# Hybrid encoder on one Trainium2 core: first transfers from two queues, the first slice split on ACT and VectorE, the second layer's first chunks in two passes, new ranks

## The chip, the cores and the metric

The kernel runs on one core of a Trainium2 chip. The metric is the device time of one execution in microseconds. Five engines work side by side, each with its own in-order list of instructions: TensorE (PE, with its weight loads shown apart as PEld), VectorE (DVE), ScalarE (ACT), GpSimd (POOL) and SyncE (SP), which here only issues DMAs. They wait for each other through semaphores.

## The reference

The trunk has two layers, called layer 0 and layer 1 below, on x of 512 positions by 1024 features, float32. Each layer does this:

```python
h = rmsnorm(x, g_attn[l])
proj = jnp.einsum('bsd,dc->bsc', h, w_in[l])            # 2304 columns
qa, ka, va, qb, kb, vb = jnp.split(proj, offs, axis=-1)
...  # q, k: RMSNorm by head, then rotary
ya = windowed_gqa_sink(qa, ka, va, sink[l])              # 8 q heads, 2 kv heads, dim 64, +-128
yb = diff_attention(qb, kb, vb, lam)                     # 4 heads, two softmaxes each
yb = rmsnorm(yb, subln[l]) * (1.0 - lambda_init)
y = jnp.concatenate([ya.reshape(B, S, SWA_Q), yb.reshape(B, S, DIFF_V)], axis=-1)
x = x + jnp.einsum('bsm,md->bsd', y, w_out[l])
h = rmsnorm(x, g_ffn[l])
gate, val = jnp.split(jnp.einsum('bsd,df->bsf', h, w_up[l]), 2, axis=-1)
gate = centred_dwconv(gate, conv_w[l], conv_b[l])        # width 3
x = x + jnp.einsum('bsf,fd->bsd', jax.nn.silu(gate) * val, w_down[l])
```

## The kernel before

**Arithmetic.** Every operand of a product is kept as two float32r parts: hi is a rounded copy (made by ACT), lo is what is left (made by VectorE, a few halves by GpSimd). A product is three matmuls, hi·hi, hi·lo and lo·hi, added up in one PSUM bank (`mm3`). This holds for activations and for weights, so each weight unit that arrives by DMA into a `wr` buffer (two of them) is cast by ACT into a `wh` buffer and subtracted into a `wl` buffer (three of each).

**Layout.** x lies transposed in SBUF as eight slices x0 to x7 of 128 features by 512 positions. `Norm.add` makes hi and lo of slice k, scaled by the norm's gain (`na_h`, `na_l`; in the feed-forward half `nf_h`, `nf_l`). The norm's 1/rms per position is applied later, to the product's result; `Norm.squares` adds up the squares of the eight slices (ACT squares, VectorE or GpSimd adds, `na_sum`), and `Norm.rms` makes the factor from it with four small matmuls (`na_ss`), VectorE and GpSimd.

**Stages of a layer.** The input projection is cut into nine chunks of 256 columns (`CHUNKS`, line 30). The first two, akv (keys and values of group A) and aq0, are made together by `first_product`: for each slice k it multiplies all four blocks of 128 positions into four PSUM banks (`pj_akq`), so that it can begin when the first slice and the first part of the weight are there. The other chunks come one after another (`project`): for two pairs of position blocks, all eight slices. Each q or k chunk then passes through `qk_track` and `qk_out`: ACT evacuates the bank (`raw_`), squares it, VectorE reduces, GpSimd takes a power, the rotary steps follow (VectorE in group A, GpSimd in group B), TensorE transposes (`tr_`, into the one bank `at`), and ACT and VectorE copy the two parts out. Group A's attention has eight steps (`sc_a` scores, softmax on VectorE and ACT, `pt_a` transposes of the weights, `pv_a`), group B's sixteen (`sc_b`, `wt_b`, `yb`, then `ss_yb` and `rt_yb` for its norm). The output projection (`wo`) runs in three passes, each adding its bank to x on VectorE (`add_x`), which frees the bank. The feed-forward half follows in two parts (`up`, `dn`).

**The order of the work.** The program order of every engine is made by a planner, `Machine`. Each piece of work is a Python generator ("track") that yields instructions or conditions. The planner holds a model of each engine's free time (`Op.cost`) and of when each operand is ready (`when`, with `NEAR` as the time from a result to a reader on TensorE or GpSimd), and puts next the instruction that could start earliest; among those within a small margin the lowest rank wins. The ranks are in `RK`: "w" weight casts (three values, by how many units are ready), "x" and "xl" the residual adds, "evac" the evacuation of projections, "kv", "qka", "qkb" the q and k tracks, "a" and "b" the attention groups, "bn" group B's norm, "nsq" the squares of the feed-forward norm. The projections and products of the main line (`filler`) have rank 1000, so that TensorE takes attention work when it is ready and projections else.

**The start.** `loads` issues on SP: `cols` (the gains and other parameters by column), then x0, the first part of w_first, x1, the second part, and so on in turn to x7, then the identity, the next weights, the rotary table, the mask and the row parameters. TensorE meanwhile does two float32 warm-up matmuls. On ACT, `first_norm` makes `na_h` of slice 0, `squares` its square, and `first_weights` the cast of the weight's first part (`wh_f`); VectorE makes `na_l` and `wl_f`.

Almost all instructions are issued on one helper line (`put`, line 248 before, 250 after), so the rows of the profile are told apart by tile names.

Of the kernel before, what the change touches and what calls it, by code (L numbers as in the profile page):

```python
# [17 lines left out]
P = 128  # L18
# [11 lines left out]
CHUNKS = ("akv", "aq0", "bq0", "bv0", "aq1", "bk0", "bv1", "bk1", "bq1")  # L30
# [4 lines left out]
AQ_TAGS = ("mm", "at")  # L35
HOLD = 0.05
SWITCH = {True: 0.2, False: 0.085}
NEAR = {"PE": 0.2, "POOL": 0.079}
# [5 lines left out]
RK = {"w": (25, 45, 4), "qkb": (8, 1), "x": 25, "xl": 18, "a": 400, "b": 12, "evac": 1, "qka": 1, "kv": 36,  # L44
      "bn": -2, "nsq": 36, "av": -4, "bv": -4}


class Op:
# [16 lines left out]
    def cost(self, writes, reads):  # L65
# [80 lines left out]
class Machine:  # L146
# [73 lines left out]
    def put(self, op, start):  # L220
# [10 lines left out]
        if op.eng == "SP":  # L231
# [46 lines left out]
class Queue:  # L278
# [13 lines left out]
def kernel(  # L292
# [96 lines left out]

    def w_load(first):  # L390
# [7 lines left out]
    def w_high(first):  # L398
        for i in range(first, len(units)):
            src, (k, n), kind = units[i]  # L400
            yield lambda: len(raws) > i
            yield m.room("wh")
            hi = new("wh", f"wh{i}", [P, k, n])
# [3 lines left out]
    def w_low(first):  # L407
        for i in range(first, len(units)):
            src, (k, n), kind = units[i]
            yield lambda: len(his) > i  # L410
            yield m.room("wl")
            lo = new("wl", f"wl{i}", [P, k, n])
# [9 lines left out]
            ready.append((hi, lo))  # L422
# [22 lines left out]
    class Norm:  # L445
# [7 lines left out]
        def add(self, k):  # L453
# [3 lines left out]
            yield act.activation(self.hi[k], x_sb[k], AF.Copy, scale=g)  # L457
# [85 lines left out]
    def first_product(l, norm, on_banks):  # L543
        banks = []
        for k in range(NK):
            if l == 0:
                yield m.has(f"fw{k}")
            if k % 2 == 0:
                yield unit_there
                w = next_unit()  # L550
            yield m.has(f"{norm.name}{k}")
            for t in range(NT):
                if k == 0:
                    yield roomy(FIRST_TAGS)
# [774 lines left out]
```

## Time and profile before

| what | value |
|---|---|
| median of 3 runs | 1201.58 us (1200.91 to 1202.31) |
| the profiled execution | 1201.83 us |
| its span, first to last instruction | 1200.0 us |
| granted clock, mean over the span | 0.998 |
| chain that ended last | PE 87%, DVE 9%, ACT 2%, POOL 1%, issue 1% |

A row of the timeline has start and duration in us, the engine, the line, the operation, out<-in, the shapes, and xN where N instructions were merged; in brackets stands how long the engine was idle before, and what ended that. A row of the waits has who waited for whom, the total in us, the number of waits and the longest. Matmuls overlap in the records, so one lasts longer than the distance to the next; the rate is read from distances. In rows by stretch of time, each engine has its busy time and its count.

### The profile page before, as it was taken

What the parts mean: (1) busy time and instruction counts of PE and PEld (TensorE: products, weight loads), DVE (VectorE), ACT (ScalarE), POOL (GpSimd) and SP (SyncE); (2) the same over time, 40 slices, a digit from 0 to 9 for tenths busy, and PEclk for the clock granted to TensorE, in tenths of its full rate; (3) what the DMA queues carried; (4) which work ended last, traced back from release to release, by engine and by line L of the source; (5) the groups of instructions that cost most, each with busy time, mean ns of one, the idle gap of its engine ahead of it and who ended that gap; (6) DMA issues with size and microseconds to landing.
All of it is one profiled execution on the core that took longest, in us unless ns stands there. A gap on an engine that the chain in (4) does not pass through costs nothing.

```text
span 1200.0 us, 16742 instructions
## 1 busy us (share of the span) xinstructions
PE 1185.3 (99%) x6452; PEld 1008.6 (84%) x6452; DVE 739.8 (62%) x1329; ACT 556.9 (46%) x977; POOL 226.6 (19%) x282
## 2 busy tenths in 40 slices
PE   8999999999999999999999999999999999999998
PEld 6998988888888888888888899888888888888887
DVE  6887799775554335454458877897755533455532
ACT  5587766454333123333436777665433321233321
POOL 2614360111100000111235144501111100011000
PEclk9999999999999999999999999999999999999999
DMA  6221121132322233322332111211323223323232
GB/s 223 71 71 36 54 71 36 54 106 88 106 84 91 93 119 91 103 84 80 103 116 69 53 54 36 71 53 36 123 88 106 81 91 97 118 89 106 76 117 87
DMA packets 33327, 102.90 MB, mean 86 GB/s; under 512 B 3936, under 2 KB 4192, under 8 KB 33248
## 3 DMA queue, kind: packets, MB, share of 16 engines
q1 hardware_dynamic: 33248, 101.84, 27.2%
q8 instruction: 50, 0.82, 0.3%
q14 instruction: 29, 0.24, 0.1%
HBM read 99.73 MB, written 2.10 MB: 85 GB/s over the span
## 4 chain that ended last, share of the span: by engine, by line
PE 87%; DVE 9%; ACT 2%; POOL 1%; issue 1%; DMA 0%; SPq 0%; DVEq 0%; ACTq 0%; POOLq 0%
PE up L248 40%; PE dn L248 20%; PE wo L248 5%; PE pj_akq L248 3%; PE pj_bk L248 3%; PE pv_a L248 2%; PE sc_b L248 2%; PE pj_aq L248 2%; PE pj_bq L248 2%; PE yb L248 1%; PE pt_a L248 1%; DVE wl L248 1%; PE pj_bv L248 1%; DVE mx_b L248 1%; PE sc_a L248 1%; PE wt_b L248 1%
## 5 line engine op out<-in xcount | busy, mean ns | idle before, releaser
L248 ACT CAST wh<-wr 128x1024 fp32r<-128x1024 f32 (+2 forms) x200 | 193.3, 966 | 378.6 <-PE up L248 183.9
L248 DVE TENSOR_TENSOR wl<-wr,wh 128x512 fp32r<-128x512 f32 (+3 forms) x240 | 230.1, 967 | 110.0 <-ACT wh L248 109.8
L248 PE MATMUL up<-nf_h,wh 128*128 128x512 f32 x704 | 274.3, 390 | 0.0
L248 PE MATMUL up<-nf_h,wl 128*128 128x512 f32 x704 | 273.9, 389 | 0.0
L248 PE MATMUL up<-nf_l,wh 128*128 128x512 f32 x704 | 273.9, 389 | 0.0
L248 PE MATMUL dn<-act,wh 128*128 128x512 f32 x704 | 216.8, 389 | 0.0
L248 POOL TENSOR_TENSOR cv<-cv,rb 128x512 f32<-128x512 f32 x44 | 57.6, 1309 | 521.3 <-ACT cv L248 521.3
L248 PEld LDWEIGHTS dn<-act,wh 128*128 128x128 f32 x704 | 132.2, 188 | 27.4
L248 PEld LDWEIGHTS up<-nf_h,wh 128*128 128x128 f32 x704 | 132.2, 188 | 27.3
L248 PEld LDWEIGHTS up<-nf_h,wl 128*128 128x128 f32 x704 | 132.2, 188 | 27.3
L248 PEld LDWEIGHTS up<-nf_l,wh 128*128 128x128 f32 x704 | 132.2, 188 | 27.2
L248 PE MATMUL dn<-act,wl 128*128 128x512 f32 x352 | 136.9, 389 | 0.0
L248 DVE TENSOR_TENSOR gp<-up,rb 128x512 f32<-128x512 f32 x44 | 30.4, 693 | 109.7 <-PE up L248 106.2
L248 DVE TENSOR_TENSOR cv<-cv,up 128x512 f32<-128x512 f32 x44 | 30.2, 687 | 83.4 <-POOL gp L248 79.0
L248 PEld LDWEIGHTS dn<-act,wl 128*128 128x128 f32 x352 | 66.1, 188 | 13.7
L248 DVE SCALAR_TENSOR_TENSOR cv<-gp,cols,cv 128x512 f32<-128x512 f32 x88 | 66.6, 761 | 5.3 <-ACT cv L248 0.9
L248 DVE TENSOR_TENSOR x<-x,dn 128x512 f32<-128x512 f32 x32 | 22.0, 687 | 74.1 <-PE dn L248 74.1
L248 ACT ACTIVATE cv<-cv 128x512 f32<-128x512 f32 x44 | 27.8, 632 | 83.7 <-DVE cv L248 83.6
L248 ACT ACTIVATE e_b<-sc_b,mx_b,rqb 128x512 f32<-128x512 f32 x64 | 49.7, 784 | 10.2 <-DVE mx_b L248 9.6
L248 ACT ACTIVATE so_a<-so_a,ng_a,rqa 128x256 f32<-128x256 f32 (+1 forms) x64 | 41.4, 651 | 11.6 <-DVE ng_a L248 11.6
L248 DVE TENSOR_REDUCE mx_b<-sc_b 128x2 f32<-128x1024 f32 x32 | 38.1, 1217 | 3.8 <-PE sc_b L248 3.7
L248 PE MATMUL pj_bv<-wh,na_h 128*128 128x256 f32 x128 | 37.8, 295 | 0.2 <-ACT raw_bq L248 0.2
(213 smaller groups left out, 2191.0 us busy)
## 6 DMA issues: line engine op xcount, KB each, us to landing
wr<-w_up SPq DMA_DIRECT2D x88, 512.0 KB, 3.5
wr<-w_in SPq DMA_DIRECT2D x28, 512.0 KB, 3.5
wr<-w_down SPq DMA_DIRECT2D x32, 384.0 KB, 3.0
wr<-w_down SPq DMA_DIRECT2D x32, 320.0 KB, 2.8
wr<-w_out SPq DMA_DIRECT2D x16, 512.0 KB, 3.5
x<-xT SPq DMA_DIRECT2D x8, 256.0 KB, 5.2
prob_f<-w_first SPq DMA_DIRECT2D x8, 256.0 KB, 5.2
wr<-w_first SPq DMA_DIRECT2D x4, 512.0 KB, 3.4
```

The source lines that it names most:

```text
L248: getattr(self.raw[op.eng], op.name)(*op.args, **op.kw)
```

## The change

- The DMA of the first part of the first weight is issued by ACT, ahead of its table load; SP issues x0 first, then `cols`, then the rest as before. The planner now takes 0.45 us for a DMA issue on any engine (0.33 before, on SP).
- The high part of slice 0 is made by VectorE (`tensor_scalar`) instead of ACT.
- In layer 0 the square of slice k waits, in the planner, for the split weight part k.
- In the first two slices of layer 0's first product, the matmuls are ordered by part (hi·hi of all four blocks, then hi·lo, then lo·hi) instead of by block.
- In layer 1 the first product goes through the slices twice: first for position blocks 0 and 1, then for 2 and 3. Its four weight units are held until the second pass has read them.
- The third and fourth weight units of each layer lie in `pair` buffers (which hold the q and k chunks later) instead of `wh` and `wl`.
- Chunk bq0 moves from third to seventh; the chunk aq1 may no longer use the bank `at`.
- NEAR for TensorE goes from 0.2 to 0.053 us, and most of the ranks change.

```diff
-CHUNKS = ("akv", "aq0", "bq0", "bv0", "aq1", "bk0", "bv1", "bk1", "bq1")
+CHUNKS = ("akv", "aq0", "bv0", "aq1", "bk0", "bv1", "bq0", "bk1", "bq1")
-AQ_TAGS = ("mm", "at")
+AQ_TAGS = ("mm",)
-NEAR = {"PE": 0.2, "POOL": 0.079}
+NEAR = {"PE": 0.053, "POOL": 0.079}
-RK = {"w": (25, 45, 4), "qkb": (8, 1), "x": 25, "xl": 18, "a": 400, "b": 12, "evac": 1, "qka": 1, "kv": 36,
-      "bn": -2, "nsq": 36, "av": -4, "bv": -4}
+RK = {"w": (25, 45, 4), "qkb": (39, 1), "x": 2, "xl": 8, "a": 60, "b": 1, "evac": 60, "qka": 12, "kv": 4,
+      "bn": 4, "nsq": 42, "av": -4, "bv": -2}
...
+        if self.name == "dma_start":
+            return 0.45, 0.0
...
+    def w_tag(i, tag):
+        return "pair" if i % (len(units) // depth) in (2, 3) else tag
...
-            yield act.activation(self.hi[k], x_sb[k], AF.Copy, scale=g)
+            if self.first and k == 0:
+                yield dve.tensor_scalar(out=self.hi[k], in0=x_sb[k], scalar1=g, scalar2=None, op0=ALU.mult)
+            else:
+                yield act.activation(self.hi[k], x_sb[k], AF.Copy, scale=g)
...
-                yield m.has(f"{self.name}{k}")
+                yield m.has(f"{self.name}{k}", *([f"fw{k}"] if self.first else []))
...
     def loads():
+        first_w.append(new("prob", "prob_f0", [P, 2, S], F32))
+        yield act.dma_start(first_w[0][:, 0], units[0][0][:, 0])
+        yield sync.dma_start(x_sb[0], x_v[:, 0])
+        yield sync.dma_start(cols[:, :, :N_COL], col_par)
         yield act.activation(warm, ones, AF.Copy, scale=ones)
-        yield sync.dma_start(cols[:, :, :N_COL], col_par)
+        m.flags.add("x0")
         for k in range(NK):
+            if k == 0:
+                continue
...
     def first_product(l, norm, on_banks):
-        banks = []
-        for k in range(NK):
...
+        w = []
+        for blocks in ((0, 1, 2, 3),) if l == 0 else ((0, 1), (2, 3)):
+            banks = []
+            for k in range(NK):
+                if blocks[0] == 0:
...
+                        w.append(next_unit())
...
+                for v in zip(*ops) if l == 0 and k < 2 else ops:
+                    yield Batch(list(v))
+                if blocks[-1] == NT - 1 and k % 2:
+                    done_with(u)
+            for i in range(0, len(blocks), 2):
+                on_banks(banks[i:i + 2], blocks[i] // 2)
```

More of the change, by code (lines that the diff above doesn't have):

```diff
@@ L401, in w_high @@
             yield lambda: len(raws) > i
-            yield m.room("wh")
-            hi = new("wh", f"wh{i}", [P, k, n])
+            th = w_tag(i, "wh")
+            yield m.room(th)
+            hi = new(th, f"wh{i}", [P, k, n])
             yield act.copy(hi, raws[i])
@@ L410, in w_low @@
             yield lambda: len(his) > i
-            yield m.room("wl")
-            lo = new("wl", f"wl{i}", [P, k, n])
+            tl = w_tag(i, "wl")
+            yield m.room(tl)
+            lo = new(tl, f"wl{i}", [P, k, n])
             raw, hi = raws[i], his[i]
@@ L432, in done_with @@
     def done_with(u):
-        m.drop("wh", u[0])
-        m.drop("wl", u[1])
+        m.drop(u[2], u[0])
+        m.drop(u[3], u[1])
     def mm3(acc, a, b, start, stop):
@@ L531, in first_weights @@
             if k % 2 == 0:
-                yield m.room("wh")
-                yield m.room("wl")
-                u = (new("wh", f"wh_f{k}", [P, 2, S]), new("wl", f"wl_f{k}", [P, 2, S]))
+                th, tl = w_tag(k // 2, "wh"), w_tag(k // 2, "wl")
+                u = (new(th, f"wh_f{k}", [P, 2, S]), new(tl, f"wl_f{k}", [P, 2, S]), th, tl)
                 ready.append(u)
-            hi, lo = (v[:, k % 2] for v in u)
+            hi, lo = (v[:, k % 2] for v in u[:2])
             yield act.copy(hi, raw[:, k % 2])
@@ L543, in first_product @@
     def first_product(l, norm, on_banks):
-        banks = []
-        for k in range(NK):
[L546 to L554, printed above, removed]
-                    banks.append(any_bank(f"pj{l}_akq_{t}", FIRST_TAGS))
-                yield from mm3(banks[t][2], (norm.hi[k][:, t * P:(t + 1) * P], norm.lo[k][:, t * P:(t + 1) * P]),
-                               (w[0][:, k % 2], w[1][:, k % 2]), k == 0, k == NK - 1)
-                if k == NK - 1 and t % 2:
-                    on_banks(banks[t - 1:t + 1], t // 2)
-            if k % 2:
-                done_with(w)
+        w = []
[3 more added lines that the diff above has]
+                if blocks[0] == 0:
+                    if l == 0:
+                        yield m.has(f"fw{k}")
+                    if k % 2 == 0:
+                        yield unit_there
+                        w.append(next_unit())
+                    yield m.has(f"{norm.name}{k}")
+                u = w[k // 2]
+                ops = []
+                for i, t in enumerate(blocks):
+                    if k == 0:
+                        yield roomy(FIRST_TAGS)
+                        banks.append(any_bank(f"pj{l}_akq_{t}", FIRST_TAGS))
+                    ops.append([pe.matmul(banks[i][2], lhsT=a[k][:, t * P:(t + 1) * P], rhs=u[j][:, k % 2],
+                                          start=n + k == 0, stop=n == 2 and k == NK - 1)
+                                for n, (a, j) in enumerate(((norm.hi, 0), (norm.hi, 1), (norm.lo, 0)))])
+                for v in zip(*ops) if l == 0 and k < 2 else ops:
[4 more added lines that the diff above has]
+                on_banks(banks[i:i + 2], blocks[i] // 2)
     def warm_up():
```

10 lines of the change are left out of this document (5 added, 5 removed).

## The prediction

> **What bounds the kernel now.** I read the page first, then the busy time by stage, then the waits of TensorE, then the timelines of the three places where it waits. The page, and two of the stages (span, then busy time and count of PE, PEld, DVE, ACT, POOL, then granted clock, DMA share, GB/s):
>
> ```profile
> span 1200.0 us, 16742 instructions
> PE 1185.3 (99%) x6452; PEld 1008.6 (84%) x6452; DVE 739.8 (62%) x1329; ACT 556.9 (46%) x977; POOL 226.6 (19%) x282
> ...
> 31.50:240.50 209.00, 206.42 (x1522) 185.29 (x1521) 177.70 (x421) 138.58 (x306) 70.42 (x57) 1.00 0.18 55
> 240.50:601.40 360.90, 360.90 (x1602) 299.16 (x1601) 181.37 (x226) 131.28 (x169) 39.53 (x73) 1.00 0.31 96
> ```
>
> TensorE has work from end to end. The feed-forward stage of layer 0, 360.9 us, has no gap, the change leaves its order alone, and layer 1's is its copy. So a time can change only by three things: the time before the first product, the clock during it, and the moments at which TensorE stands still in the attention stages. The change alters no count of matmuls. All named waits of TensorE, with their totals:
>
> ```profile
> PE pj_akq L248 <- ACT wh_f L248: 2.1, 1, 2.1
> PE wo L248 <- DVE x L248: 2.1, 3, 0.8
> PE tr_ka L248 <- DVE qal L248: 1.4, 1, 1.4
> PE pt_a L248 <- DVE p_a L248: 1.3, 4, 0.4
> PE tr_bq L248 <- POOL raw_bq L248: 1.2, 2, 1.0
> PE warm_up L248 <- POOL unit L358: 1.0, 1, 1.0
> PE rt_yb L248 <- POOL rr_yb L248: 0.5, 2, 0.3
> PE pj_akq L248 <- DVE wl_f L248: 0.2, 1, 0.2
> PE pj_bv L248 <- ACT raw_bq L248: 0.2, 1, 0.2
> PE tr_qa L248 <- DVE ka L248: 0.2, 1, 0.2
> ```
>
> Without the first product's two and the warm-up's, 6.9 us of waits remain; that is all that "ranks anew", the chunk order and the two passes can win between them. The start, in order of time:
>
> ```profile
> 0.73 1.28 ACT L248 ACT_TABLE_LOAD   x1 [0.73 <-PEq L1325]
> 0.74 0.67 SPq L248 DMA_DIRECT2D cols<-col_par  x1
> 0.95 3.48 PE L248 MATMUL warm_up<-unit 128*128 128x512 f32 x4 [0.95 <-POOL unit L358]
> 1.46 0.58 SPq L248 DMA_DIRECT2D x<-xT  x1
> 2.09 0.42 SPq L248 DMA_DIRECT2D prob_f<-w_first  x1
> 4.76 0.72 ACT L248 ACTIVATE na_h<-x,cols 128x512 fp32r<-128x512 f32 x1 [2.44 <-DMA x<-xT]
> 5.39 0.61 ACT L248 ACTIVATE na_sum<-x 128x512 f32<-128x512 f32 x1
> 5.91 0.60 ACT L248 CAST wh_f<-prob_f 128x512 fp32r<-128x512 f32 x1
> 6.54 0.69 DVE L248 TENSOR_TENSOR wl_f<-prob_f,wh_f 128x512 fp32r<-128x512 f32 x1 [0.28 <-ACT wh_f L248]
> 6.56 0.51 PE L248 MATMUL pj_akq<-wh_f,na_h 128*128 128x512 f32 x1 [2.14 <-ACT wh_f L248]
> 7.29 0.71 PE L248 MATMUL pj_akq<-wl_f,na_h 128*128 128x512 f32 x1 [0.22 <-DVE wl_f L248]
> ...
> 547.05 54.40 PE dn L248 x240
> ```
>
> Three ACT steps stand in a row (the slice's high part, its square, the weight's cast) before the first matmul at 6.56. The last row gives the pitch of a 512-column matmul, 54.40 / 240 = 0.227 us.
>
> **The change part by part.** *The start.* ACT and DVE before:
>
> ```order
> L248 ACT_TABLE_LOAD
> L248 ACTIVATE unit<-unit 128x1
> L248 ACTIVATE na_h_104<-x_66,cols 128x512
> L248 ACTIVATE na_sum<-x_66 128x512
> L248 CAST wh_f_105<-prob_f_100 128x512
> ```
>
> ACT now; x_66 and prob_f_82 are the first slices of x and of the weight:
>
> ```order
> L250 DMA prob_f_82<-w_first 128x512
> L250 ACT_TABLE_LOAD
> L250 ACTIVATE unit<-unit 128x1
> L250 CAST wh_f_105<-prob_f_82 128x512
> L250 ACTIVATE na_sum<-x_66 128x512
> ```
>
> DVE now, from its first instruction:
>
> ```order
> L250 TENSOR_TENSOR wl_f_106<-prob_f_82,wh_f_105 128x512
> L250 TENSOR_SCALAR na_h_104<-x_66,cols 128x512
> L250 SCALAR_TENSOR_TENSOR na_l_121<-x_66,cols,na_h_104 128x512
> L250 SCALAR_TENSOR_TENSOR na_l_138<-x_67,cols,na_h_124 128x512
> L250 TENSOR_TENSOR wl_f_106<-prob_f_82,wh_f_105 128x512
> ```
>
> The high part moved from ACT to DVE, but behind the weight's low part: "at once" is in truth cast, low part, high part. When the data come is bounded by these answers (min, median, max to landing, of x, the first weights and cols):
>
> ```profile
> DMA to landing us min/median/max: 3.2/5.2/5.8
> ...
> DMA to landing us min/median/max: 3.4/5.2/5.9
> ...
> DMA to landing us min/median/max: 2.5/2.5/2.5
> ...
> 3.50:4.00 0.50, 0.50 (x2) 0.00 (x0) 0.00 (x0) 0.00 (x0) 0.00 (x0) 1.00 1.07 377
> ```
>
> The weight is issued at 0.73 by ACT instead of at 2.09; its landing is bounded by 3.2 and 3.9 us behind that (3.4, the least of its own rows, plus 0.5 for sharing: 256 KB at 377 GB/s is 0.7 us, and x is under way at the same time). I take 4.2. Cols, now second on SP at about 1.4, land 2.5 to 3.4 later, by 4.8. Then cast 0.60 to 4.85, low part 0.69 to 5.5. The high part on DVE, with a scalar per partition, has no row of its shape before: a 128x512 product of another form took 0.69 (wl_f above), so 0.3 to 0.69; I take 0.45, nearer its simpler arithmetic. First matmul at about 6.0 against 6.56: **-0.56** (0 if data come 0.6 later, -0.9 if 0.3 earlier). The four high matmuls and then the four with the low part fill 8 x 0.227 = 1.8 us, in which the slice's low part is made, so the stall from 6.56 to 7.29 (0.73 - 0.227 = 0.50) is gone: **-0.50**. The squares held back cost nothing: the sum of squares moves from behind 54 product matmuls to behind 66, and its readers, the evacuations at the end of the first product, come 30 matmuls (6.8 us) later still. ACT's new DMA issue (0.42 to 0.67 by SP's rows) puts its table load 0.7 later, to end at 2.7, before any data.
>
> The Trainium skill ("Trainium Kernel Development and Optimization", Key Constraints) says that DMAs of several queues share the same 16 DMA engines and interleave, so that a second queue saves only issue time. That speaks against a gain from two queues; by it only the one issue, 0.42 us, would be won, and my 0.56 stands mostly on the dropped ACT steps.
>
> *The clock.*
>
> ```profile
> 7.00:7.50 0.50, 0.28 (x2) 0.21 (x2) 0.24 (x2) 0.50 (x2) 0.00 (x0) 0.91 1.22 266
> 7.50:8.00 0.50, 0.50 (x2) 0.40 (x2) 0.50 (x1) 0.50 (x2) 0.00 (x0) 0.50 0.90 262
> ...
> 10.00:11.00 1.00, 1.00 (x4) 0.81 (x3) 1.00 (x3) 1.00 (x3) 0.00 (x0) 0.59 1.05 406
> ```
>
> A mean of 0.91 over the first half microsecond is 0.09 us at half speed, one of 0.59 over the last row's microsecond 0.82 us: the clock was at half from 7.41 to 10.82, 3.41 us, of which half, 1.7 us, was lost. It follows the gap between the warm-up's end (0.95 + 3.48 = 4.43) and 6.56. Now that gap is 1.6 us, not 2.1. Whether it still trips the clock no row decides; the ends are 0 and -1.7, I take the middle: **-0.85**.
>
> *Layer 1's first chunks in two passes.* Before, the first 16 us of its attention stage held these:
>
> ```profile
> 622.24 0.47 ACT L248 ACTIVATE raw_ka<-pj_akq,na_r 128x256 f32<-128x256 f32 x1 [2.36 <-PE pj_akq L248]
> ...
> 628.28 0.68 DVE L248 TENSOR_TENSOR raw_qa<-raw_qa,sq_qa 128x512 f32<-128x512 f32 x1
> ...
> 631.80 0.44 PE L248 MATMUL tr_ka<-ident,raw_ka 128*128 128x128 f32 x2 [1.41 <-DVE qal L248]
> 646.87 0.66 PE L248 MATMUL tr_bq<-ident,raw_bq 128*128 128x128 f32 x4 [1.01 <-POOL raw_bq L248]
> ```
>
> TensorE there before (pj_bq the third chunk, tr_qa and tr_ka the transposes of the first two):
>
> ```order
> L248 MATMUL tr_qa_0_5853<-ident,raw_qa_0_5777 128x128 x4
> L248 MATMUL pj_bq_0_5792<-wh_5750,na_h_5555 128x256
> L248 MATMUL pj_bq_0_5792<-wl_5755,na_h_5555 128x256
> L248 MATMUL pj_bq_0_5792<-wh_5750,na_l_5560 128x256
> L248 MATMUL pj_bq_0_5792<-wh_5750,na_h_5626 128x256
> L248 MATMUL pj_bq_0_5792<-wl_5755,na_h_5626 128x256
> L248 MATMUL pj_bq_0_5792<-wh_5750,na_l_5632 128x256
> L248 MATMUL tr_ka_0_5886<-ident,raw_ka_0_5775 128x128 x2
> ```
>
> And now, inside the second pass of the first product (pj_akq):
>
> ```order
> L250 MATMUL tr_qa_0_5784<-ident,raw_qa_0_5722 128x128 x4
> L250 MATMUL pj_akq_5719<-wh_5580,na_h_5453 128x512
> L250 MATMUL pj_akq_5719<-wl_5625,na_h_5453 128x512
> L250 MATMUL pj_akq_5719<-wh_5580,na_l_5460 128x512
> L250 MATMUL pj_akq_5718<-wh_5580,na_h_5504 128x512
> L250 MATMUL pj_akq_5718<-wl_5625,na_h_5504 128x512
> ```
>
> From evacuation to the last step of raw_qa took 622.24 to 628.96, 6.7 us, with 1.2 us of two weight pieces in it; now one piece and a short ka step stand there, so about 6.5. TensorE has 27 matmuls of the second pass, 6.1 us, before it needs it, and the evacuation begins some 0.4 us before the pass ends: a wait of 0 to 0.3. Between the two transposes stand 15 matmuls, 3.4 us, instead of 0.7, so the bank that qal frees is there in time: the 1.41 goes. Chunk bq0, whose steps run on POOL, is now seventh, with a chunk of other matmuls ahead of its transposes: tr_bq's 1.2 goes. Together **-2.6**. No matmul is added, since both passes do half the blocks each. The two passes hold four weight units longer; two of them lie in "pair" buffers, and the next chunk's first unit still finds its slot, so nothing new waits on weights.
>
> *Ranks.* The three wo waits, one of them here:
>
> ```profile
> 172.07 2.38 DVE L248 TENSOR_TENSOR wl<-wr,wh 128x512 fp32r<-128x512 f32 x2
> 174.37 0.67 DVE L248 TENSOR_TENSOR x<-x,wo 128x512 f32<-128x512 f32 x1
> 175.09 0.50 PE L248 MATMUL wo<-yh,wh 128*128 128x512 f32 x1 [0.81 <-DVE x L248]
> ```
>
> The residual add that frees a bank stood behind two weight pieces. DVE there before, around the add of wo_0_1:
>
> ```order
> L248 TENSOR_TENSOR wl_b_0_2_2262<-wt_b_0_2_2263,wh_b_0_2_2261 128x4x128
> L248 SCALAR_TENSOR_TENSOR mx_b_1_2_2278<-mx_b_1_2_2278,rqb_87 128x2
> L248 SCALAR_TENSOR_TENSOR mx_b_1_3_2279<-mx_b_1_3_2279,rqb_87 128x2
> L248 TENSOR_TENSOR wl_2242<-wr_2140,wh_2186 128x512 x2
> L248 TENSOR_TENSOR x_67<-x_67,wo_0_1_2219 128x512
> ```
>
> And now:
>
> ```order
> L250 TENSOR_REDUCE mx_b_2_1_2350<-sc_b_2_1_2336 128x2
> L250 TENSOR_TENSOR wl_b_1_2_2316<-wt_b_1_3_2359,wh_b_1_2_2315 128x4x128
> L250 TENSOR_TENSOR x_67<-x_67,wo_0_1_2296 128x512
> L250 SCALAR_TENSOR_TENSOR mx_b_2_0_2349<-mx_b_2_0_2349,rqb_88 128x2
> L250 SCALAR_TENSOR_TENSOR mx_b_2_1_2350<-mx_b_2_1_2350,rqb_88 128x2
> L250 TENSOR_TENSOR wl_2383<-wr_2265,wh_2380 128x512 x2
> ```
>
> With its rank from 25 to 2 (18 to 8 in the last pass) the add goes ahead of both weight pieces, 2.38 us, more than any wo wait: **-2.1** (0 if DVE is as late by its other work). What is pushed back is a weight piece that is first read at wo_0_6, behind four wo groups of 12 matmuls (48 x 0.227 = 10.9 us). Of the other waits (pt_a 1.3, rt_yb 0.5, and 0.4), half: **-1.1**. New waits are certain in kind and unknown in place, since all handovers to TensorE have moved: bounds 0 and 6.9 (the old sum again), taken **+1.2**, a sixth, because three of the old causes are removed by more room and not by luck.
>
> Sum: -0.56 - 0.50 - 0.85 - 2.6 - 2.1 - 1.1 + 1.2 = -6.5. The profiled execution took 1201.83 us (span 1200.0 and 1.83 around it), so 1195.4; it lies 0.25 above the median of the three runs, so **1195.2** for a median.
>
> **The rivals.** *The clock stays full.* The gap of 1.6 us is too short to trip it: 0.85 more is won, 1194.4. For: the gap shrinks by a quarter. Against: it did trip after 2.1. By the Trainium skill ("TensorE: Matmul & The Clock Gate", Part 1) the clock is set by free-running windows of about 3.4 us, so the same kernel may be hit or not; the trace's 3.41 us agrees. Part of the forecast's own range; chance 0.22.
>
> *The waits are conserved.* DVE is busy 177.7 of 209 us in layer 0's attention; putting the add first only delays another producer, and the 2.1 + 1.1 come back at softmax handovers: -6.5 + 3.2 = -3.3, 1198.3. For: that 85%. Against: b-scores now start before more projections are used up. Chance 0.17.
>
> *The start wins nothing.* The change doesn't do there what it says: weight and x share the DMA engines, cols come last, and the first matmul stays at 6.56 with a slow clock; with the waits conserved, -0.5 - 2.6 + 1.2 = -1.9, 1199.7, within 0.2% (about what a measurement tells from no change). Chance 0.11.
>
> *Slower: the closer lead.* The assumed time from a result to TensorE falls from 0.2 to 0.053 us, so each handover is placed 0.147 us later in need. By the order there are some 80 handovers a layer (20 groups of pt_a, 16 of scores, 16 of wt_b, and the rest), 160 in all; from 61 of them exposed, 9.0 us, the sum is slower by over 0.2%; two thirds exposed cost 15.7, less 6.5: +9.2, 1210.8. Against: the first matmul began 0.05 us after ACT's cast ended, so 0.053 is near the truth. Chance 0.06.
>
> *Everything goes.* All 6.9 of waits, the start's 0.9 and 0.5 and the clock's 1.7: -10.0, 1191.6. Chance 0.08.
>
> **How the numbers follow.** Forecast 0.36, clock 0.22, conserved 0.17, no start 0.11, all 0.08, slower 0.06. Faster by over 0.2% (below 1199.2): 0.36 + 0.22 + 0.17 + 0.08 less 0.02 from the conserved case's upper end, 0.81; slower 0.06; the same 0.13. Forecast and clock case alone span 1193 to 1197.5; with the conserved case above and the full gain below, 1191 to 1199.6.
>
> **What would show it.** First matmul near 6.0 without a stall before its second; a shorter or absent half-clock stretch; no wait at layer 1's tr_ka and tr_bq; tr_qa inside the second pass of pj_akq waiting under 0.3; no wo wait behind a weight piece. Wrong: named waits of TensorE still near 7 us in total, or many of 0.1 to 0.2 us at pt_a and wt_b.

## The result, and the profile after

The new kernel takes **1206.8 us** (median, 1205.98 to 1209.7) where before takes 1201.24 us (1199.29 to 1202.31) beside it: a ratio of 1.0051, interval 1.0038 to 1.0064. Half a per cent was lost where 1195.2 us and a gain were forecast. The profiled execution took 1209.7 us, the upper end of its range. Single executions far above the others of their kernel (1226.73 us in r_start, which is the profiled one, and 2349.69 in a_near) are in none of the ratios below.

The page, and the stages by stretch of time (attention of layer 0 from the first matmul of the third chunk, its feed-forward half, then layer 1 from its first product to its feed-forward half; columns as in the prediction):

```profile
span 1207.6 us, 16734 instructions
PE 1190.7 (99%) x6452; PEld 1008.9 (84%) x6452; DVE 741.2 (61%) x1327; ACT 556.0 (46%) x976; POOL 224.0 (19%) x285
```

```profile
31.16:245.76 214.60, 209.04 (x1521) 184.47 (x1520) 178.74 (x415) 137.54 (x306) 73.02 (x63) 1.00 0.16 50
245.76:606.69 360.93, 360.93 (x1602) 299.39 (x1601) 181.56 (x227) 131.40 (x169) 39.59 (x73) 1.00 0.31 96
606.69:842.70 236.01, 231.12 (x1625) 204.41 (x1624) 186.61 (x436) 147.19 (x318) 73.50 (x67) 0.99 0.19 61
```

And the same two attention stretches of before, cut at the same matmuls:

```profile
31.50:240.37 208.87, 206.29 (x1522) 185.16 (x1521) 177.57 (x420) 138.45 (x306) 70.42 (x57) 1.00 0.18 55
601.29:835.11 233.82, 228.82 (x1626) 204.00 (x1625) 188.36 (x435) 147.12 (x318) 78.85 (x68) 1.00 0.20 61
```

The matmuls are the same in number, and VectorE and ACT are busy as long within 1.8 us. The span grew by 7.6 us, and that is the sum of the stages: start 31.50 to 31.16, -0.34; layer 0's attention 208.87 to 214.60, **+5.73**; the feed-forward half unchanged; layer 1 233.82 to 236.01, **+2.19**. The waits of TensorE by name (total, number, longest):

```profile
PE tr_qa L250 <- DVE raw_qa L250: 2.5, 1, 2.5
PE wt_b L250 <- DVE wl_b L250: 2.3, 3, 0.9
PE pj_akq L250 <- DVE na_h L250: 1.7, 1, 1.7
PE pt_a L250 <- DVE p_a L250: 1.6, 5, 0.5
...
PE pt_a L250 <- DVE so_a L250: 0.7, 3, 0.4
PE pt_a L250 <- DVE bk0l L250: 0.7, 1, 0.7
PE wt_b L250 <- DVE bq0l L250: 0.5, 1, 0.5
PE pt_a L250 <- DVE bq0l L250: 0.4, 1, 0.4
PE wo L250 <- DVE x L250: 0.4, 2, 0.2
PE wt_b L250 <- DVE bk1l L250: 0.2, 1, 0.2
```

Against before, wo on x fell from 2.1 to 0.4, and tr_ka on qal, tr_bq on raw_bq and rt_yb are gone. In their place stand tr_qa with 2.5, wt_b with 3.0 in three rows and pt_a on new partners with 1.8. Without the start the named waits are 9.3 us, before 6.9.

That is 2.4 us more, while the two attention stretches grew by 7.9, so the names do not cover the loss. By the rows above, 2.98 of layer 0's 5.73 us are time in which TensorE has no matmul in the records (214.60 less 209.04, against 208.87 less 206.29), and 2.75 are busy time of the same matmuls. In layer 1 the time without a matmul did not grow at all (4.89 against 5.00); the busy time grew by 2.30, of which 1.7 is the clock (see below). Stops hide in the busy time, because a 128x256 matmul lasts 0.28 us in the records while the next one begins 0.12 us after it: by an estimate from these two numbers, a named wait behind such a matmul is 0.16 us shorter than the stop, and a shorter stop has no row.

The start, ACT, VectorE and TensorE:

```profile
0.73 0.41 ACTq L250 DMA_DIRECT2D prob_f<-w_first  x1
...
4.58 0.62 ACT L250 CAST wh_f<-prob_f 128x512 fp32r<-128x512 f32 x1 [1.82 <-DMA prob_f<-w_first]
...
5.23 0.69 DVE L250 TENSOR_TENSOR wl_f<-prob_f,wh_f 128x512 fp32r<-128x512 f32 x1 [5.23 <-ACT wh_f L250]
5.83 0.48 DVE L250 TENSOR_SCALAR na_h<-x,cols 128x512 fp32r<-128x512 f32 x1
...
6.46 2.04 PE L250 MATMUL pj_akq<-wh_f,na_h 128*128 128x512 f32 x4 [1.73 <-DVE na_h L250]
...
8.31 1.91 PE L250 MATMUL pj_akq<-wl_f,na_h 128*128 128x512 f32 x4
```

The order on VectorE is as foreseen (low part, then high part), and the wait ahead of the second group of matmuls is gone. But the first matmul begins at 6.46, and its group of four needs 1.85 us to the next, 0.46 each against the pitch of 0.227: half speed.

The head of layer 1, on ACT and TensorE:

```profile
617.26 1.05 ACT L250 CAST wh<-wr 128x1024 fp32r<-128x1024 f32 x1 [5.56 <-DMA wr<-w_in]
618.33 1.28 ACT L250 ACT_TABLE_LOAD   x1
620.50 0.20 ACT L250 ACTIVATE lexp<-ldot 128x2 f32<-128x2 f32 x1 [0.89 <-DVE ldot L250]
620.61 0.46 ACT L250 ACTIVATE raw_ka<-pj_akq,na_r 128x256 f32<-128x256 f32 x1
...
627.38 0.63 PE L250 MATMUL tr_qa<-ident,raw_qa 128*128 128x128 f32 x4 [2.54 <-DVE raw_qa L250]
```

ACT stands between the end of the first pass (its 48 matmuls from 606.69 on, 10.9 us, end not before 617.6) and the evacuation at 620.61 with a weight's cast, a table load and the exponential for lambda, which itself waits for VectorE. Behind the 2.54 us the clock (last but two columns) falls to half:

```profile
628.00:632.00 4.00, 4.00 (x13) 3.10 (x12) 2.65 (x6) 0.58 (x1) 0.00 (x0) 0.57 0.61 197
632.00:636.00 4.00, 4.00 (x26) 3.38 (x26) 0.49 (x2) 2.33 (x7) 0.00 (x0) 1.00 0.17 66
```

A mean of 0.57 over 4 us is 3.4 us at half speed, of which half, 1.7 us, is lost: 13 matmuls in the first row, 26 in the next.

### The profile page after: what moved, and what is told of

It is laid out like the page before. It is cut to its first block, busy times and chain, and to the rows that moved or that the text cites. A ratio compares the mean times of both kernels' runs of the same rounds, so it can differ in the third digit from the quotient of the medians.

```text
span 1207.6 us, 16734 instructions
## 1 busy us (share of the span) xinstructions
PE 1190.7 (99%) x6452; PEld 1008.9 (84%) x6452; DVE 741.2 (61%) x1327; ACT 556.0 (46%) x976; POOL 224.0 (19%) x285
## 4 chain that ended last, share of the span: by engine, by line
PE 81%; DVE 9%; ACT 7%; issue 1%; DMA 1%; ACTq 0%; DVEq 0%; SPq 0%
PE up L250 40%; PE dn L250 20%; PE wo L250 6%; PE pj_akq L250 3%; ACT so_a L250 2%; PE pj_bv L250 2%; PE pj_bk L250 2%; PE yb L250 2%; PE pj_bq L250 1%; DVE mx_b L250 1%; DVE so_a L250 1%; PE sc_b L250 1%; DVE wl L250 1%; ACT e_b L250 1%; ACT wh L250 1%
## 5 line engine op out<-in xcount | busy, mean ns | idle before, releaser
L250 DVE TENSOR_TENSOR wl<-wr,wh 128x512 fp32r<-128x512 f32 (+3 forms) x237 | 224.0, 958 | 105.5 <-ACT wh L250 104.9
L250 DVE TENSOR_TENSOR x<-x,wo 128x512 f32<-128x512 f32 (+1 forms) x64 | 34.7, 550 | 8.5 <-PE wo L250 8.1
```

Of the source, the lines that this page charges most:

```text
L250: getattr(self.raw[op.eng], op.name)(*op.args, **op.kw)
```

## The experiments

In layer 0's attention the change undoes and does several things at once, so the first four kernels set one table back, or set one table alone. Theory 1 is the closer lead (NEAR), theory 2 the ranks, theory 3 the order of the chunks.

Every kernel below that the planner orders anew (these four, a_pass, b_near21 and b_near19) carries one more edit, which the diffs leave out: two buffers are asked for in one condition instead of one after the other (`tmp` and `sc` of group B's scores, in the kernels with the new code also `wh` and `wl` of the first weights). It is not what acts: with before's numbers, with the new kernel's, and on before's code with each lead tried below, the planner lays out the same program with it and without it.

**u_near**: the new kernel with the old lead.

```diff
-NEAR = {"PE": 0.053, "POOL": 0.079}
+NEAR = {"PE": 0.2, "POOL": 0.079}
```

> The changed kernel with one number put back: the planner's assumed time from a result to TensorE is 0.2 us again, not 0.053. Theory 1 (the closer lead: an order without slack, in which every handover that comes a little late stops TensorE): layer 0's attention, 214.6 us in the changed kernel and 209.0 in the one before, falls to 209 to 211, the named waits of TensorE there from 6.6 us to under 4, and the time is 1200 to 1203. Theory 2 (the ranks) and theory 3 (the chunk order): layer 0's attention stays above 213 and the time above 1205. The start and the wait at layer 1's tr_qa (2.5 us) stay by all theories unless the order there changes.

1207.91 us, ratio 1.0055 (1.0038 to 1.0071). Layer 0's attention 211.69 us, 2.9 less than the new kernel's, and tr_qa waits 0.7 instead of 2.5; but layer 1 takes 237.18, 1.2 more, with more waits of pt_a. The whole gains nothing.

**a_near**: before with the new lead alone.

```diff
-NEAR = {"PE": 0.2, "POOL": 0.079}
+NEAR = {"PE": 0.053, "POOL": 0.079}
```

> The kernel before with only that number changed, 0.2 to 0.053 us. Theory 1: layer 0's attention grows from 209.0 us to 212 or more, with small waits at pt_a and wt_b, and the time is 1204 to 1210. Theories 2 and 3: it stays within 1.5 us of 209.0 and the time within 1199 to 1203.

1221.31 us, ratio 1.0162 (1.0145 to 1.0179): 20 us. Layer 0's attention 217.79, layer 1 242.66. Half of that is a single kind of wait, not many small ones, and at each of its two places the granted clock was at half for 3.4 us:

```profile
PE wt_b L248 <- DVE mx_b L248: 9.5, 2, 4.8
```

**u_rank**: the new kernel with the old ranks.

```diff
-RK = {"w": (25, 45, 4), "qkb": (39, 1), "x": 2, "xl": 8, "a": 60, "b": 1, "evac": 60, "qka": 12, "kv": 4,
-      "bn": 4, "nsq": 42, "av": -4, "bv": -2}
+RK = {"w": (25, 45, 4), "qkb": (8, 1), "x": 25, "xl": 18, "a": 400, "b": 12, "evac": 1, "qka": 1, "kv": 36,
+      "bn": -2, "nsq": 36, "av": -4, "bv": -4}
```

> The changed kernel with the ranks of before. Theory 2 (the new ranks, the evacuations' 60 above all, make the producers late): layer 0's attention falls from 214.6 us to 209 to 211 and the time to 1200 to 1203. Theory 1: it stays at 213 or more, time 1205 or more. Layer 1's tr_qa wait may move with the order by either.

1216.33 us, ratio 1.0123 (1.0107 to 1.0138); layer 0's attention 219.28.

**u_chunks**: the new kernel with the old order of chunks.

```diff
-CHUNKS = ("akv", "aq0", "bv0", "aq1", "bk0", "bv1", "bq0", "bk1", "bq1")
+CHUNKS = ("akv", "aq0", "bq0", "bv0", "aq1", "bk0", "bv1", "bk1", "bq1")
-AQ_TAGS = ("mm",)
+AQ_TAGS = ("mm", "at")
```

> The changed kernel with the chunk order and the banks for aq1 of before (bq0 third). Theory 3 (the chunk order, which takes GpSimd's chain from the head of the stage and crowds the group B chunks into its middle): layer 0's attention falls to 211 or less and the time to 1203 or less. Theories 1 and 2: it stays at 213 or more; layer 1's first waits (tr_ka, tr_bq, 2.6 us before) may come back.

1224.28 us, ratio 1.0195 (1.018 to 1.021); layer 0's attention 225.19. So no table, taken back alone, gives back the loss, and two of the three make it worse. (In u_chunks the clock was at half for 13.7 us of that stretch, which makes up 6.8 of the 10.6 us by which it is longer than the new kernel's.) As single causes theories 1, 2 and 3 all fall.

For the next kernels the planner's choices were written down once and are replayed from a list, so that single instructions can be moved and every other one keeps its place on its engine. In the diffs below a space marks what stays.

**r_start**: before's order with the new start alone. The new code hands the banks of the first product over for evacuation only when all four blocks are done; before's earlier hand-over of the first two is kept here.

```diff
 (ACT)
+DMA prob_f<-w_first
 ACT_TABLE_LOAD
-ACTIVATE na_h<-x,cols 128x512
-ACTIVATE na_sum<-x 128x512
 CAST wh_f<-prob_f 128x512
+ACTIVATE na_sum<-x 128x512
 (VectorE)
+TENSOR_TENSOR wl_f<-prob_f,wh_f 128x512
+TENSOR_SCALAR na_h<-x,cols 128x512
 SCALAR_TENSOR_TENSOR na_l<-x,cols,na_h 128x512
-TENSOR_TENSOR wl_f<-prob_f,wh_f 128x512
...
```

> Before's order of instructions, given as a list, with only the start replaced by the new one (two queues, first slice split, squares held back, products by part). Single places (theory A): the start is worth what the new kernel's profile shows for it, the third chunk beginning at about 31.2 instead of 31.50 us, and nothing else moves: 0.3 us faster, a ratio of 0.9997. The prediction's own steps for the start: 1.9 us faster, 0.9984. Conserved waits (theory B): the earlier start meets the same later waits, 1.0000.

1200.6 us beside 1201.44, ratio 0.9992 (0.9983 to 1.0002). As a median the start is worth 0.8 us; the interval takes in no change.

**r_adds**: before's order, one VectorE instruction moved in each layer.

```diff
 SCALAR_TENSOR_TENSOR mx_b<-mx_b,rqb 128x2
+TENSOR_TENSOR x<-x,wo 128x512
 TENSOR_TENSOR wl<-wr,wh 128x512 x2
-TENSOR_TENSOR x<-x,wo 128x512
```

> Before's order, given as a list, with two instructions moved: the residual add of the second block of the output projection, in each layer, goes ahead of the two weight pieces on VectorE that it stood behind. Single places (theory A): the two waits of wo on it, 0.81 and 0.79 us, go and nothing else changes: 1.6 us faster, a ratio of 0.9987. Conserved waits (theory B): the weight pieces come 0.7 us later and the waits show up behind them; within 0.3 us of before.

1201.63 us, ratio 0.9999 (0.999 to 1.0008): nothing. The two waits of wo went, and 1.1 us came back at once in each layer. The place in layer 0, VectorE, GpSimd and TensorE:

```profile
172.06 0.67 DVE L302 TENSOR_TENSOR x<-x,wo 128x512 f32<-128x512 f32 x1
172.09 3.00 POOL L302 TENSOR_TENSOR wl<-wr,wh 128x512 fp32r<-128x512 f32 x2 [0.28 <-ACT wh L302]
172.66 2.98 DVE L302 TENSOR_TENSOR wl<-wr,wh 128x512 fp32r<-128x512 f32 x2
175.94 0.68 DVE L302 TENSOR_TENSOR wl_b<-wt_b,wh_b 128x512 fp32r<-128x512 f32 x1
176.77 0.63 PE L302 MATMUL tr_bq<-ident,raw_bq 128*128 128x128 f32 x4 [1.08 <-DVE wl_b L302]
```

The add goes first, but the two weight pieces now begin 0.57 us behind GpSimd's two instead of together with them, and take 2.98 us instead of 2.38 (GpSimd's 3.00 instead of 3.50); wl_b ends 0.6 us later than before, and TensorE, 0.8 us earlier, waits for it.

**v_head**: the new kernel's order; in layer 1 the table load and the exponential (ACT) go behind the evacuations and squares of the first two chunks, and the exponential's reader nlam one place back on VectorE.

```diff
-ACT_TABLE_LOAD
-ACTIVATE lexp<-ldot 128x2
 ACTIVATE raw_ka<-pj_akq,na_r 128x256
...
 ACTIVATE sq_ka<-raw_ka 128x256
+ACT_TABLE_LOAD
+ACTIVATE lexp<-ldot 128x2
```

> The new kernel's order, given as a list, with one thing moved: in layer 1 the exponential of the lambda setup (ACT, with its table load) and its reader go behind the evacuations of the first two chunks. Single places (theory A): the evacuation begins 2.1 us earlier, the wait of tr_qa falls from 2.5 to about 0.4 and the clock does not fall to half behind it (1.7 us more): layer 1 up to its feed-forward half takes 232.2 to 234 instead of 236.0 us, the whole 2 to 3.8 us less than the new kernel, a ratio to before of 1.0015 to 1.003. Conserved waits (theory B): the wait moves to the next transposes; layer 1 stays at 235.5 to 236.5, ratio 1.005.

1206.34 us, ratio 1.0042 (1.0028 to 1.0056). Layer 1 takes 233.83 us, 2.2 less, and the clock stays full; but tr_qa still waits 2.02:

```profile
621.20 0.21 DVE L303 TENSOR_SCALAR nlam<-lexp 128x1 f32<-128x1 f32 x1 [1.66 <-ACT lexp L303]
...
625.67 0.52 PE L303 MATMUL tr_qa<-ident,raw_qa 128*128 128x128 f32 x3 [2.02 <-DVE raw_qa L303]
```

The reader of the exponential (nlam) now held VectorE for 1.66 us ahead of the chain to raw_qa. The wait had moved one instruction on.

**v_dve**: the new kernel's order; six instructions of layer 0's attention, each of which TensorE waited for, moved ahead on VectorE (three) and ACT (three), TensorE's order left alone. One of them:

```diff
 TENSOR_REDUCE ss_bk<-sq_bk 128x8
+TENSOR_TENSOR wl_b<-wt_b,wh_b 128x4x128
 SCALAR_TENSOR_TENSOR mx_b<-mx_b,rqb 128x2
 TENSOR_TENSOR wl<-wr,wh 128x512
 TENSOR_SCALAR sv_bk<-ss_bk 128x8
-TENSOR_TENSOR wl_b<-wt_b,wh_b 128x4x128
```

> The new kernel's order, given as a list, with six single instructions of layer 0's attention moved ahead of others on VectorE or ACT, each the one that TensorE waited for (waits of 0.55, 0.68, 0.32, 0.44, 0.95 and 0.91 us, 3.85 together); TensorE's own order is unchanged. Single places (theory A): 3 to 3.9 us less, layer 0's attention at 211 instead of 214.6 us, a ratio to before of 1.0015 to 1.002. Conserved waits (theory B): what is pushed back becomes the next late result; layer 0's attention stays at 214 to 215, ratio 1.005.

1207.89 us, ratio 1.0047 (1.0032 to 1.0062), not to be told from the new kernel. Its named waits in layer 0's attention are 2.75 us instead of 4.90, where 3.85 were aimed at, and the stretch takes 212.82. The same order of instructions in layer 0 took 214.60 in the new kernel's profile, 213.44 in v_head's and 213.47 in v_head2's, so single profiles of one order differ by 1.2 us there, and of the 1.8 us less only 0.6 lies beyond that.

**r_adds2**: r_adds, with the next late result cleared too.

```diff
+TENSOR_TENSOR x<-x,wo 128x512
 TENSOR_TENSOR wl<-wr,wh 128x512
+TENSOR_TENSOR wl_b<-wt_b,wh_b 128x4x128
 TENSOR_TENSOR wl<-wr,wh 128x512
-TENSOR_TENSOR x<-x,wo 128x512
...
-TENSOR_TENSOR wl_b<-wt_b,wh_b 128x4x128
```

> Before's order, given as a list, with the residual add of the second output block ahead of the two weight pieces as in r_adds, and now also the value weights' low part (wl_b), for which tr_bq then waited 1.1 us, ahead of the second weight piece, in both layers. Cleared chain (theory A): a wait comes back only where the next result of the same engine is late too; with both in front the 0.81 and 0.79 us stay won: 1.6 us faster, ratio 0.9987, and no wait of tr_bq on wl_b. Conserved waits (theory B): it comes back a third time, at the next e_b or add; ratio 0.9996 to 1.0004.

1200.45 us, ratio 0.9993 (0.9984 to 1.0002). Layer 0's attention 207.77 (1.1 less than before), layer 1 233.38 (0.4 less), no wait on wl_b. As a median about half of the 1.6 stays, but the interval takes in no change, and r_best below does not bear it out; a wait of ss_yb on bq1l (0.4) is the third in the row.

**r_clear**: r_start and r_adds2 together, and three waiting transposes put later on TensorE, tr_bq of layer 1 behind three groups of projection matmuls, pt_a in each layer behind one.

```diff
-MATMUL tr_bq<-ident,raw_bq 128x128 x4
 MATMUL pj_bv<-wh,na_h 128x256
 MATMUL pj_bv<-wl,na_h 128x256
 MATMUL pj_bv<-wh,na_l 128x256
...
+MATMUL tr_bq<-ident,raw_bq 128x128 x4
```

> Before's order, given as a list, with the new start of r_start, the two places of r_adds2, and three transposes of waits 1.01, 0.43 and 0.44 us put behind three, one and one groups of three projection matmuls. Cleared chain (theory A): 0.8 (r_start's measured gain) + 1.6 + 1.9 = 4.3 us faster than before, ratio 0.9964; it beats both kernels. Conserved waits (theory B): only the start's 0.8 stays, ratio 0.9993.

1200.04 us, ratio 0.9989 (0.998 to 0.9998): 1.2 us less, no more than the start and the adds give by their medians, so a gain from the transposes is not to be seen. tr_bq, which comes 1.1 us later in TensorE's order, still waits:

```profile
PE tr_bq L304 <- POOL raw_bq L304: 1.7, 2, 1.2
```

Why its producer came later by as much was not tried.

**v_head2**: v_head, and the reader nlam behind the chain to raw_qa on VectorE.

```diff
-TENSOR_SCALAR nlam<-lexp 128x1
...
 TENSOR_TENSOR raw_qa<-raw_qa,sq_qa 128x512
 TENSOR_TENSOR raw_ka<-raw_ka,tab 128x256
+TENSOR_SCALAR nlam<-lexp 128x1
```

> The new kernel's order, given as a list, with layer 1's exponential for lambda behind the evacuations as in v_head, and now its reader on VectorE (nlam), on which VectorE stood for 1.7 us there, behind the rotary steps of the first q chunk. Cleared chain (theory A): raw_qa is done 1.5 to 2 us earlier than in v_head, tr_qa waits under 0.5, the clock stays full behind it: layer 1 up to its feed-forward half takes 231.5 to 232.5 us against 236.0 (new) and 233.8 (v_head), ratio to before 1.002 to 1.003. Conserved waits (theory B): 233.5 or more, ratio 1.004.

1205.33 us, ratio 1.0034 (1.0024 to 1.0044). The evacuation, the last step of raw_qa and the transposes:

```profile
615.26 0.47 ACT L303 ACTIVATE raw_ka<-pj_akq,na_r 128x256 f32<-128x256 f32 x1
...
621.48 0.68 DVE L303 TENSOR_TENSOR raw_qa<-raw_qa,sq_qa 128x512 f32<-128x512 f32 x1
...
622.30 0.63 PE L303 MATMUL tr_qa<-ident,raw_qa 128*128 128x128 f32 x4 [0.33 <-DVE raw_qa L303]
```

tr_qa waits 0.33 us, the clock stays full, and layer 1 takes 232.69 us: 3.3 less than in the new kernel, and 1.1 less than in before's profile (0.3 less than in that of r_start2 below, whose order there is before's). So the two passes lose nothing once the lambda setup is out of their way.

**a_pass**: the code edits (start, two passes, pair buffers) with before's chunk order, ranks and lead; the planner orders anew.

```diff
-NEAR = {"PE": 0.053, "POOL": 0.079}
+NEAR = {"PE": 0.2, "POOL": 0.079}
...
-AQ_TAGS = ("mm",)
+AQ_TAGS = ("mm", "at")
```

> Before's chunk order, ranks and lead (NEAR 0.2) with the code edits alone: the new start and the two passes with pair buffers; the planner orders anew. If the loss is the tables' (theory C): 0.8 us from the start and 1.4 from tr_ka less, ratio 0.998 to 0.9995. If two passes are themselves late (the evacuation comes behind the setup and the weight waits for pair buffers; theory D): layer 1 at 235 to 237 us instead of 233.8, ratio 1.001 to 1.003. If any new plan draws new waits (theory E): layer 0's attention, whose code is the same but for the start, moves by over 2 us from before's 208.9.

1218.62 us, ratio 1.0145 (1.0131 to 1.0159):

```profile
32.22:254.77 222.55, 212.85 (x1521) 187.49 (x1520) 179.85 (x419) 136.85 (x306) 68.00 (x58) 0.98 0.16 48
```

Layer 0's attention has before's tables here, and before's code but for the new start, the pair buffers and the later hand-over of the first product's banks, and takes 222.55 us instead of 208.87; 3.4 us of that were lost to the clock, which was at half for 6.8 us. On the new code the new tables are 12 us better than the old ones. The new tables on before's code were not tried.

**b_near21**: before, with nothing but the planner's lead changed, by 0.01 us.

```diff
-NEAR = {"PE": 0.2, "POOL": 0.079}
+NEAR = {"PE": 0.21, "POOL": 0.079}
```

> Before with nothing changed but NEAR for TensorE from 0.2 to 0.21 us, so that the planner orders anew. If a new order in itself draws new waits (theory E): layer 0's attention moves by over 1.5 us from 208.9, ratio off 1 by 0.002 or more. If the order bears small changes (theory H): within 1 us in both layers, ratio 0.999 to 1.001.

1213.68 us, ratio 1.0112 (1.0096 to 1.0127). Among its waits are these at wo, which before does not have:

```profile
PE wo L248 <- ACT yh_b L248: 3.2, 4, 0.9
...
PE wo L248 <- DVE yl_b L248: 1.8, 2, 0.9
```

```profile
31.49:246.98 215.49, 209.06 (x1521) 186.01 (x1520) 179.16 (x420) 137.25 (x306) 70.15 (x57) 0.99 0.17 53
```

**b_near19**: the same, 0.01 us the other way.

```diff
-NEAR = {"PE": 0.2, "POOL": 0.079}
+NEAR = {"PE": 0.19, "POOL": 0.079}
```

> Before with nothing changed but NEAR for TensorE from 0.2 to 0.19 us. As for b_near21: over 1.5 us in layer 0's attention by theory E, and not with the opposite sign of b_near21's change, since the lead is not what acts; within 1 us by theory H.

1216.19 us, ratio 1.0127 (1.0113 to 1.014), with the same two waits at wo (3.2 and 1.8 us in total). Its attention of layer 0:

```profile
30.93:248.33 217.40, 209.69 (x1521) 185.94 (x1520) 179.23 (x417) 137.51 (x306) 73.24 (x60) 0.99 0.17 52
```

A hundredth of a microsecond more lead costs 6.6 us in layer 0's attention, a hundredth less costs 8.5. In both, 1.7 us of that went to the clock, which was at half for 3.4 us behind one pair of the wo waits. Since either direction costs, it is not more or less lead that acts, but that the planner lays out a new order at all.

**r_start2**: r_start with one VectorE instruction moved.

```diff
+TENSOR_SCALAR na_h<-x,cols 128x512
 TENSOR_TENSOR wl_f<-prob_f,wh_f 128x512
-TENSOR_SCALAR na_h<-x,cols 128x512
```

> r_start (before's order given as a list, with the new start) with one VectorE instruction moved: the high part of the first slice stands ahead of the weight's low part, so that it runs beside ACT's cast. If VectorE's order held the first matmul (theory F): it begins at 5.3 to 5.6 us instead of 6.5, 0.9 to 1.2 us more than r_start wins, ratio to before 0.9983. If the slice or the gains land late (theory G): it stays at 6.3 to 6.5, ratio 0.9992.

1198.26 us beside 1200.98, ratio 0.998 (0.9972 to 0.9989). The first matmul comes at 5.67, the matmuls run at full speed from there (the second group of four follows after 1.00 us), and the third chunk begins at 28.48. The attention stretches, in before's order, take 208.29 and 233.00 us, 0.6 and 0.8 less than in before's profile.

**r_best**: r_start2 and the two places of r_adds2, on VectorE:

```diff
+TENSOR_SCALAR na_h<-x,cols 128x512
 TENSOR_TENSOR wl_f<-prob_f,wh_f 128x512
-TENSOR_SCALAR na_h<-x,cols 128x512
...
+TENSOR_TENSOR x<-x,wo 128x512
 TENSOR_TENSOR wl<-wr,wh 128x512
+TENSOR_TENSOR wl_b<-wt_b,wh_b 128x4x128
 TENSOR_TENSOR wl<-wr,wh 128x512
-TENSOR_TENSOR x<-x,wo 128x512
```

> r_start2 with the two places of r_adds2. The gains add (theory A): 0.8 + 0.8 as measured for r_start and r_adds2, and 1.0 for the first matmul: 2.6 us faster than before, ratio 0.9978, faster than both kernels. If the gains do not add: 0.9985 to 0.9990.

1198.47 us, ratio 0.9978 (0.9969 to 0.9987): faster than both kernels, and not to be told from r_start2: the attention stretches take 208.23 and 233.21 us, so the two places won nothing that can be seen here. That the ratio is the one expected is luck, since the start won what the two places did not. Its start:

```profile
5.00 0.49 DVE L304 TENSOR_SCALAR na_h<-x,cols 128x512 fp32r<-128x512 f32 x1 [5.00 <-DMA cols<-col_par]
...
5.64 1.17 PE L304 MATMUL pj_akq<-wh_f,na_h 128*128 128x512 f32 x4 [0.91 <-DVE na_h L304]
```

The high part runs beside ACT's cast, held only by the landing of cols, and the third chunk begins at 28.45 us instead of 31.50.

## Why the prediction was wrong, point by point

**The bound.** That TensorE has work from end to end and only its stops can change held: the feed-forward half is 360.93 us against 360.92, and the whole difference of 7.6 us lies in the start and the two attention stretches.

**The step that failed: "new waits ... taken +1.2".** The prediction listed the waits of before and asked which of them each edit removes. Most of that came true: wo 2.1 to 0.4, tr_ka's 1.4 and tr_bq's 1.2 gone. (The sum as written gives 1195.1, not 1195.2, which changes nothing.) What failed was the other side. The waits at new partners (tr_qa 2.5, wt_b 3.0, pt_a 1.8) are 7.3 us, above even the bound of 6.9, and that bound was no bound: it was the sum of before's waits, as if a new order could be no worse than the old. With the waits that went, the terms came to 4.6 us less; measured were 2.4 us more in the named waits and 7.9 in the two stretches, the clock's 1.7 and the hidden part of the stops included. b_near21 and b_near19 show what a new order is: the same work, laid out by the same planner with the same ranks, take 6.6 and 8.5 us more in layer 0's attention (1.7 of each by the clock) and 5.1 and 6.6 more in layer 1. Over the orders measured here layer 0's attention takes 208.9 (before), 211.7, 214.6 (the new kernel), 215.5, 217.4, 217.8, 219.3, 222.6 and 225.2 us. Before is the lowest of them, and the new kernel lies among the others. For "all handovers to TensorE have moved" the orders measured would have given a range of 0 to +16 us in that stretch alone.

**The slower rival** ("the closer lead") had the sign and some of the size (1210.8 against 1206.8), but its mechanism is not shown. With the old lead (u_near) layer 0 gives back 2.9 us and layer 1 loses 1.2 more, and the whole is no faster; and in before 0.01 us in either direction costs more than 0.147 us per handover was to cost here. A closer lead did do harm in one kernel, a_near, and there by one kind of wait of up to 4.8 us rather than by many of 0.1 to 0.2.

**"The waits are conserved"** is the rival that came nearest to what moved instructions do. r_adds is its proof in one place: 1.6 us of waits taken out, 2.1 put in one instruction further on. v_head2 shows its limit: with the next late result cleared as well, 3.3 us stayed won in layer 1. In r_adds2 half of the 1.6 stayed as a median, which its interval does not tell from nothing.

**The two passes.** Of the step "a wait of 0 to 0.3" at tr_qa the chain was right, 6.6 us from the evacuation at 620.61 to the end of raw_qa at 627.23 (6.5 foreseen). Wrong was "the evacuation begins some 0.4 us before the pass ends": it began 2.5 to 3 us behind it, because ACT had the setup of lambda with its table load in between. v_head2 shows this: the same two passes without it wait 0.33. In before, ACT stood idle for 2.36 us ahead of its evacuation at 622.24, waiting for TensorE, so the setup was out of the way by then. "Nothing new waits on weights" was wrong too: the cast at 617.26 waited 5.56 us for a transfer of w_in; but in v_head the evacuation followed such a cast directly, so this cost little. The stop then cost the clock (1.7 us), which no term held: the step looked for a half-clock stretch at the start alone. By the Trainium skill ("TensorE: Matmul & The Clock Gate", Part 1) an idle window of about 3.4 us turns the clock down; here the stop that did it lasted 2.54 us (2.24 in v_dve, where the clock fell too, while 2.02 in v_head left it full), so by the traces it takes less. In b_near21 two stops of 0.93 and 0.91 us, with half a microsecond of matmuls between them, were followed by 3.4 us at half the clock as well.

**The start.** The first matmul came at 6.46 instead of 6.0. The weight's part was there at 4.58, inside the bounds (up to 4.6) but not at the 4.2 taken, and the high part behind the low part took the rest. r_start2 shows that this order, which the prediction had read from the program and then passed by, was the larger half: with the high part in front the first matmul begins at 5.67, 0.8 us earlier, where the new start as it is won 0.1. The stall before the second matmul is gone, as foreseen, but not to be seen as time, since the matmuls ran at half speed.

**The clock at the start.** Its two ends (0 and -1.7) were right, and the middle is no case: the same start ran at half speed in the new kernel's profile and at full speed in r_clear's, with gaps of 1.73 and 1.77 us ahead of it:

```profile
6.50 1.17 PE L304 MATMUL pj_akq<-wh_f,na_h 128*128 128x512 f32 x4 [1.77 <-DVE na_h L304]
...
7.51 1.08 PE L304 MATMUL pj_akq<-wl_f,na_h 128*128 128x512 f32 x4
```

The next group follows after 1.01 us here and after 1.85 there; the column of the granted clock shows 1.00 in both, so that here the distances tell the clock and the column does not. The third chunk begins at 29.34 here and at 31.16 there, 1.8 us apart. Over all profiles a gap of 1.37 us (b_near19) was followed by half speed and one of 1.92 (v_head2) was not. The free-running windows of the Trainium skill ("TensorE: Matmul & The Clock Gate", Part 1), cited in the prediction, agree: the gap alone does not decide.

**What stays open.** Which property of an order makes it good was not found. Each wait has its late instruction, and its neighbours on VectorE, ACT and GpSimd are late with it; the runs show that clearing one place outside the head of layer 1 won at most about half of its wait, not why before's order has fewer such places. Whether before's numbers had been picked for the time of their order is not on record, and no run puts the new tables on before's code or tries them with other leads than the two.

## What to carry to other kernels

Where a planner lays out the whole program, an edit's first effect can be a new order, and its price is the spread between orders, to be measured by a change of the planner that should do nothing (here 0.01 us of lead: 13 to 15 us). Only then do the edit's own microseconds count; to test those, hold the order fixed and move single instructions. And ask of every wait that goes what is the next late result on the same engine, since that is where it can come back, in r_adds the whole of it.

## What the runs showed of the hardware

A VectorE instruction beside a GpSimd one can take more than twice as long. Two places of the new kernel's layer 0, the second just ahead of a wait of TensorE:

```profile
88.06 1.82 DVE L250 TENSOR_SCALAR so_a<-so_a,rl_a 128x256 f32<-128x256 f32 x2
88.45 1.28 POOL L250 TENSOR_TENSOR raw_bk<-raw_bk,sq_bk 128x512 f32<-128x512 f32 x1
...
217.01 1.87 DVE L250 SCALAR_TENSOR_TENSOR e_b<-e_b,al_b,e_b 128x512 f32<-128x512 f32 x1
217.04 1.29 POOL L250 TENSOR_TENSOR wl<-wr,wh 128x512 fp32r<-128x512 f32 x1
218.81 0.68 DVE L250 TENSOR_TENSOR wl_b<-wt_b,wh_b 128x512 fp32r<-128x512 f32 x1
219.54 0.65 PE L250 MATMUL wt_b<-ident,e_b 128*128 128x128 f32 x4 [0.91 <-DVE wl_b L250]
```

And the second place in v_head, whose order in layer 0 is the same:

```profile
216.99 0.74 DVE L303 SCALAR_TENSOR_TENSOR e_b<-e_b,al_b,e_b 128x512 f32<-128x512 f32 x1
217.02 1.86 POOL L303 TENSOR_TENSOR wl<-wr,wh 128x512 fp32r<-128x512 f32 x1
```

e_b began with GpSimd's instruction and ends 0.55 us behind its end; the same form takes 0.74 us alone (at 175.94 in before). The two so_a, of which each takes 0.42 us elsewhere even with 384 columns (at 122.83 and 123.24), end 0.15 us behind GpSimd's. The two weight pieces of r_adds took 2.98 us behind GpSimd's, against 2.38 in before, where both pairs began at 172.07 and GpSimd's was the longer one (3.50 us, in r_adds 3.00). In v_head it is the other way round: e_b takes 0.74 us and GpSimd's instruction 1.86 instead of 1.29. Both pairs of starts lie 0.03 us apart, with VectorE's first, so which of the two is held up differs between executions of one order. In v_head TensorE has no wait behind e_b; the 0.91 us of it are most of the 1.2 us by which single profiles of this order differ in layer 0. By the Trainium skill ("SBUF — State Buffer", Who interferes with whom) the two engines share a port pair that one of them holds for a whole instruction while the other waits; the rows agree. It makes an instruction's time depend on what another engine does, and with it every lead that an order rests on.
